# First stage of a one-layer transformer kernel: a load in two pieces, three weight subtractions on GpSimd, one subtraction later

## The chip, the cores and the metric

The kernel runs on one core of a Trainium2 chip. The metric is the device time of one execution in microseconds (us). Before the change it was 2847.78 us, the median of 3 runs (2846.89, 2847.78 and 2852.01 us).

The core has five engines with a queue of instructions each, and each queue runs strictly in its own order: PE (matrix products; PEld is its loading of weights), DVE (vector), ACT (scalar), POOL (GpSimd) and SP, which here issues all the DMA transfers. An instruction waits for semaphores of the engines or transfers that it depends on.

## The reference, cut to what matters

The program computes one layer: 2048 tokens of width 1024, stick-breaking attention with 16 heads, then a SwiGLU feed-forward network. Shift, scale and gate of each half come from a conditioning vector c.

```python
mod_all = jnp.einsum('bd,lde->lbe', jax.nn.silu(c), ada_w) + ada_b[:, None]
sh_m, sc_m, gt_m, sh_f, sc_f, gt_f = jnp.split(mod_all[i][:, None, :], 6, axis=-1)
h = modulate(rms_norm(x, norm_g[i, 0]), sh_m, sc_m)      # h * (1 + sc) + sh
y = stick_breaking_mixer(h, sb_w_qkv[r], sb_w_o[r])      # starts with h @ w_qkv
x = x + gt_m * rms_norm(y, norm_g[i, 1])
h = modulate(rms_norm(x, norm_g[i, 2]), sh_f, sc_f)
y = swiglu_ffn(h, ffn_w_in[i], ffn_w_out[i])
x = x + gt_f * rms_norm(y, norm_g[i, 3])
```

The change lies in the very beginning: the first shift and scale (`sh_m`, `sc_m`), the first 512 rows of `h`, and their product with the first 128 columns each of the q, k and v weights.

## The kernel before

All products are done to float32 accuracy by splitting each operand into a high part (rounded to the matrix engine's format) and a low part (the operand less its high part). `mm3` (lines 153 to 157) makes each product of three matmuls: high by high (L155), high weights by low activations (L156), low weights by high activations (L157). So every product needs two conversions, which ACT does, and two subtractions.

The first stage handles the first block of 512 tokens while the modulation vectors that it needs are themselves still being computed. Shift and scale (1024 values each) come in four pieces q = 0 to 3, each 256 values of both. A piece is a sum over 8 chunks of the conditioning vector, k = 0 to 7.

- Loads. `ada_chunk(q, kh)` loads the weights of piece q for half the chunks (kh = 0: chunks 0 to 3; kh = 1: chunks 4 to 7), 1 MB in one transfer of 8 KB per partition; piece 2 comes in eight transfers of 256 KB. `load_weights` loads a 128x1024 block of qkv weights (512 KB); t = 1, 0, 2 in the order of use (k, q, v).
- Sums. `ada_sum` (L639 for the first chunk, L642 for the others) adds one chunk times its value of c into `asum` on DVE. Chunk 7 (and chunk 0 of piece 0) skips DVE: `ada_direct` (L652) lets PE add it into the piece's accumulator `acol`; `ada_rest` (L659) lets PE add the columns of `asum`. `ada_cols_done` (L667, L669, L670) then makes `shift` and `g_eff` on DVE.
- First weights. `weights_high(t)` (L680) converts on ACT, `weights_low(t)` (L685) subtracts on DVE.
- First activations. `x_turn` transposes tile m of the normalised x on PE (L315). `full_high(m)` applies shift and scale on ACT (L701, tile `hf`) and converts it (L705, the high half of tile `ht`). `low(m)` subtracts (L710, the low half of `ht`) and, for odd m, puts the pair of tiles on a list of stores to `h_s`; these stores are issued at L405, during the next product but one.
- Products. `first_products(m, ts)` multiplies tile m with the weights t in `ts`; the order is 1, 0, 2.

The loop over q (from line 761) does for q = 0: begin piece 1, sum its chunks 0 to 6 on DVE, sum the first two chunks of piece 2, then on PE the products of tile 0, transposes, the direct and rest sums of piece 1, the products of tile 1, and last `ada_cols_done(1)` and `full_high` of tiles 2 and 3. For q = 1 and 2 the low parts of tiles 2q and 2q + 1 are put between the sums.

The queues of PE, ACT, DVE and POOL run in the order in which the program writes them. SP's order is the scheduler's. SP has eight semaphores for its transfers and uses them in turn, so a transfer is issued only when the one eight places before has landed.

Of the kernel before, what the change touches and what calls it, by code (L numbers as in the profile page):

```python
# [12 lines left out]
ALU = mybir.AluOpType  # L13
# [6 lines left out]
KC = D // P  # L20
# [61 lines left out]
def f32(ap):  # L82
    return ap.bitcast(F32)
# [3 lines left out]
def hybrid_trunk_kernel(  # L87
# [15 lines left out]
    nc = tc.nc  # L103
# [67 lines left out]
    def sb(shape, dtype, **kw):  # L171

        return (odd if kw["tag"] in ODD_TAGS else att).tile(shape, dtype, **kw)
# [3 lines left out]
    raws = {}  # L177

    def load_weights(p, t, tag="wraw"):
        raw = sb([P, KC, P], F32, name=f"wr{p}_{t}", tag=tag, bufs=BUFS[tag])  # L180
        nc.sync.dma_start(raw, wqkv[p, t])
        raws[p, t] = raw
# [110 lines left out]
    def x_load(b):  # L293
        for i in range(4):
            r0 = b * BT + i * P
            xt = sb([P, D], F32, name=f"x{b}_{i}", tag="v", bufs=BUFS["v"])
            nc.sync.dma_start(xt, x[r0 : r0 + P])
            x_tiles[b, i] = xt
# [11 lines left out]
    def x_turn(b, k):  # L310

        pool, tag = (tps, "t") if b < 2 else (accps, "acc")
        pt = pool.tile([P, BT], F32, name=f"xT{b}_{k}", tag=tag)
        for i in range(4):
            nc.tensor.transpose(  # L315
                pt[:, i * P : (i + 1) * P], x_norm[b, i][:, k * P : (k + 1) * P], ident
            )
        return pt
# [297 lines left out]
    def ada_chunk(q, kh):  # L616
        ks = range(KC // 2 * kh, KC // 2 * (kh + 1))
        if q == 2:
            for k in ks:
                w = sb([P, 2, AQ], F32, name=f"ac{q}_{k}", tag="a", bufs=BUFS["a"])  # L620
                nc.sync.dma_start(w, ada_first[q, kh][:, :, k % 4])
                chunks[q, k] = w
            return
        tag = "ht" if (q, kh) == (1, 1) else "qt"
        w = sb([P, 2, KC // 2, AQ], F32, name=f"ac{q}_{kh}", tag=tag, bufs=BUFS[tag])
        nc.sync.dma_start(w, ada_first[q, kh])
        for k in ks:
            chunks[q, k] = w[:, :, k % 4]

    def ada_begin(q):  # L630
        cols_ps[q] = zps.tile([P, BT], F32, name=f"acol{q}", tag="z")
        nc.vector.memset(cols_ps[q][:, :4], 0.0)

    def ada_sum(q, k):
        w, scale = chunks[q, k], c_act[:, k : k + 1]
        if q not in piece_sums:
            acc = sb([P, 2, AQ], F32, name=f"asum{q}", tag="w", bufs=BUFS["w"])
            piece_sums[q] = acc
            nc.vector.tensor_scalar(acc, w, scale, None, op0=ALU.mult)  # L639
        else:  # L640
            acc = piece_sums[q]
            nc.vector.scalar_tensor_tensor(acc, w, scale, acc, op0=ALU.mult, op1=ALU.add)  # L642

    def ada_sums(q):
        return [k for k in range(KC) if k not in ON_PE[q]]
# [3 lines left out]
    def ada_direct(q, k):  # L649

        for n, seg, js in COLUMNS:
            nc.tensor.matmul(  # L652
                cols_ps[q][:, n : n + 1], chunks[q, k][:, seg, js], c_act[:, k : k + 1],
                start=False, stop=False, skip_group_check=True,
            )

    def ada_rest(q):
        for n, seg, js in COLUMNS:
            nc.tensor.matmul(  # L659
                cols_ps[q][:, n : n + 1], piece_sums[q][:, seg, js], ones[:, 0:1],  # L660
                start=False, stop=n == 3, skip_group_check=True,
            )

    def ada_cols_done(q):

        ps, ms = cols_ps.pop(q), slice(2 * q, 2 * q + 2)
        nc.vector.tensor_tensor(shift[:, 0, ms], ps[:, 0:2], b_cols[:, 0, ms], op=ALU.add)  # L667
        sc = sb([P, KC], F32, name=f"sc0_{q}", tag="sc", bufs=1)[:, :2]
        nc.vector.tensor_tensor(sc, ps[:, 2:4], b_cols[:, 1, ms], op=ALU.add)  # L669
        nc.vector.scalar_tensor_tensor(  # L670
            g_eff[:, 0, ms], sc, 1.0, gc[:, 0, ms], op0=ALU.add, op1=ALU.mult
        )
# [5 lines left out]
    def weights_high(t):  # L678
        hl = sb([P, 2, KC, P], F32R, name=f"w0_{t}", tag="whl", bufs=BUFS["whl"])
        nc.scalar.copy(hl[:, 0], raws[0, t])  # L680
        weights[0, t] = hl[:, 0], hl[:, 1]

    def weights_low(t):
        hi, lo = weights[0, t]
        nc.vector.tensor_tensor(lo, raws.pop((0, t)), f32(hi), op=ALU.subtract)  # L685

    def first_products(m, ts=(1, 0, 2)):
        for t in ts:
            w = weights[0, t]
            mm3(  # L690
                first_acc[t], (w[0][:, m], w[1][:, m]),
                (first_h[m][:, 0], first_h[m][:, 1]), m == 0, m == KC - 1,
            )

    def full_high(m):
        if m % 2 == 0:
            ht = sb([P, 2, 2, BT], F32R, name=f"ht0_0_{m // 2}", tag="ht", bufs=BUFS["ht"])
            first_h.extend([ht[:, 0], ht[:, 1]])
            norm_tile[0] = ht
        full = sb([P, BT], F32, name=f"hf0_{m}", tag="tmp", bufs=BUFS["tmp"])  # L700
        nc.scalar.activation(  # L701
            full, turned_x.pop(m), AF.Identity,
            bias=shift[:, 0, m : m + 1], scale=g_eff[:, 0, m : m + 1],
        )
        nc.scalar.copy(first_h[m][:, 0], full)  # L705
        first_full[m] = full

    def low(m):
        hl = first_h[m]
        nc.vector.tensor_tensor(hl[:, 1], first_full.pop(m), f32(hl[:, 0]), op=ALU.subtract)  # L710
        if m % 2 == 1:
            stores.append((h_s[0][:, m - 1 : m + 1], f32(norm_tile[0])))
# [4 lines left out]
    nc.scalar.activation(spare, mhalf, AF.Sigmoid)  # L717
    x_load(0)
    ada_chunk(0, 0)
    ada_chunk(0, 1)  # L720
    load_weights(0, 1)
    nc.sync.dma_start(b_cols, ada_b_cols)
    nc.sync.dma_start(gc, g_cols)
    load_weights(0, 0)
    load_weights(0, 2, "qkn")
    ada_chunk(1, 0)
    ada_chunk(1, 1)
    ada_chunk(2, 0)
# [22 lines left out]
    ada_rest(0)  # L751
    weights_high(1)
    weights_low(1)
    ada_cols_done(0)
    weights_high(0)
    weights_low(0)
    weights_high(2)
    full_high(0)
    low(0)
    full_high(1)  # L760
    weights_low(2)
    low(1)


    for q in range(4):
        m = 2 * q
        if q < 3:
            if q == 0:
                ada_begin(1)
            begun = 2 if q > 0 else 0  # L770
            for n, k in enumerate(ada_sums(q + 1)[begun:]):
                ada_sum(q + 1, k)
                if q > 0 and n in (1, 3):
                    low(m + (n == 3))
            if q < 2:

                ada_begin(q + 2)
                for k in ada_sums(q + 2)[:2]:
                    ada_sum(q + 2, k)
        else:  # L780
            low(m)
            low(m + 1)
        first_products(m)
        if q < 3:
            turned_x[m + 2] = x_turn(0, m + 2)
            ada_direct(q + 1, KC - 1)
            if q == 0:
                first_products(m + 1, (1,))
            turned_x[m + 3] = x_turn(0, m + 3)
            ada_rest(q + 1)  # L790
            first_products(m + 1, (0, 2) if q == 0 else (1, 0, 2))
            ada_cols_done(q + 1)
            full_high(m + 2)
            full_high(m + 3)
        else:
            first_products(m + 1)
        if q == 1:
            load_weights(1, 1)
            load_weights(1, 0)
            x_load(1)  # L800
            load_weights(1, 2, "v")
# [595 lines left out]
    for n, (s, f) in enumerate(groups):  # L1397
# [3 lines left out]
        for at, product in enumerate(PRODUCTS):  # L1401
            acc = banks_of[{1: 0, 6: 0, 7: 0, 4: 0, 5: 1, 3: 1, 2: 2}[product]]
            for k in range(H4):
# [4 lines left out]
                t = 4 * at + k  # L1408
# [192 lines left out]
```

## Time and profile before

| | |
|---|---|
| time, median of 3 runs | 2847.78 us |
| time of the profiled execution | 2847.31 us |
| its span (first to last instruction) | 2845.1 us |
| PE busy | 2795.6 us, 98% of the span |
| DVE busy | 2028.4 us, 71% |
| ACT busy | 1632.3 us, 57% |
| POOL busy | 1277.0 us, 45% |
| DMA queue, share of 16 engines | 56.0% |
| L685 (low parts of the first weights), DVE | 3 of 128x1024, mean 1224 ns |
| L642 and L639 (sums of the pieces), DVE | 23 and 4 of 128x512 |

The profile is one execution; times in it are microseconds from the start of the span. In its timeline a row has the start, the time taken, the engine, the line, the operation, the tiles written and read (out<-in, numbers left out), the shapes, the count of merged instructions, and in brackets the idle time of the engine before it and what ended that. The profiled execution has 2.2 us outside its span.

### The profile page before, as it was taken

Reading aid. Unit: us, or ns where it says so; the run is one execution under the profiler, and the core shown is the slowest. Engines: PE = TensorE matmul, PEld = TensorE weight load, DVE = VectorE, ACT = ScalarE, POOL = GpSimd, SP = SyncE. Lnnn points to the kernel's source line nnn. Section 1 sums busy time; section 2 is a strip of 40 time slices with the busy share of each in tenths; the row PEclk is TensorE's granted clock in tenths of the full one; section 3 lists DMA queues with packets and bytes.
Section 4 is the critical chain, followed back from the end, with each engine's and each line's share of the span. In section 5 each row is a group of like instructions: output and inputs, shape, how many; then the busy total and the mean of one; then the engine's idle time right before and its main releaser. Section 6 shows DMA issues by size and latency. Waiting matters only on the chain.

```text
span 2845.1 us, 41790 instructions
## 1 busy us (share of the span) xinstructions
PE 2795.6 (98%) x13848; PEld 2333.9 (82%) x13848; DVE 2028.4 (71%) x2822; ACT 1632.3 (57%) x3265; POOL 1277.0 (45%) x2032
## 2 busy tenths in 40 slices
PE   7999999999999999999999999999999999999998
PEld 6788888888888888887888888888788888888887
DVE  6788898888888888888866766555775665133467
ACT  5787877788787877777645533333433333322243
POOL 1475666676576655656410122221222222544454
PEclk9999999999999999999999999999999999999999
DMA  8765556656665635546289645435453335545566
GB/s 329 271 211 167 189 155 227 211 170 234 189 209 192 209 118 179 196 133 231 88 299 312 203 137 152 122 98 161 130 177 108 112 107 163 191 142 155 180 214 195
DMA packets 239368, 516.84 MB, mean 182 GB/s; under 512 B 22321, under 2 KB 110385, under 8 KB 221489
## 3 DMA queue, kind: packets, MB, share of 16 engines
q1 hardware_dynamic: 239152, 514.18, 56.0%
q8 instruction: 109, 1.79, 0.3%
q14 instruction: 107, 0.87, 0.1%
HBM read 346.85 MB, written 118.49 MB: 164 GB/s over the span
## 4 chain that ended last, share of the span: by engine, by line
PE 87%; DVE 6%; ACT 2%; DMA 2%; issue 2%; POOL 1%; SPq 0%; DVEq 0%; POOLq 0%; ACTq 0%
PE s L155 9%; PE s L156 9%; PE s L157 9%; PE z L519 8%; PE o L598 8%; PE t L570 8%; PE pj L155 6%; PE pj L156 6%; PE pj L157 6%; PE o L156 4%; PE o L157 4%; PE o L155 4%; PE y L157 2%; PE y L155 2%; PE y L156 2%
## 5 line engine op out<-in xcount | busy, mean ns | idle before, releaser
L560 POOL TENSOR_TENSOR a<-a,w 128x512 f32<-128x512 f32 (+3 forms) x640 | 619.4, 968 | 217.8 <-DVE w L553 126.8
L553 DVE TENSOR_TENSOR_SCAN w<-z,c,begin 128x512 f32<-128x512 f32 x384 | 489.6, 1279 | 81.2 <-ACT z L538 61.5
L155 PE MATMUL s<-r,l 128*128 128x512 f32 x1232 | 481.4, 391 | 4.3 <-DVE p L1364 3.7
L157 PE MATMUL s<-r,l 128*128 128x512 f32 x1232 | 479.4, 389 | 0.0
L156 PE MATMUL s<-r,l 128*128 128x512 f32 x1232 | 479.3, 389 | 0.0
L536 ACT ACTIVATE a<-z 128x512 f32<-128x512 f32 (+3 forms) x640 | 347.2, 543 | 167.2 <-PE z L519 135.7
L598 PE MATMUL o<-aT,v 128*128 128x512 f32 (+3 forms) x1280 | 384.3, 381 | 0.1
L586 DVE TENSOR_TENSOR aT<-t,aT 128x512 fp32r<-128x512 f32 (+3 forms) x640 | 359.3, 596 | 22.9 <-ACT aT L580 22.2
L519 PE MATMUL z<-kt,qt 128*128 128x512 f32 (+3 forms) x1280 | 363.1, 365 | 0.0
L580 ACT CAST aT<-t 128x512 fp32r<-128x512 f32 (+3 forms) x640 | 314.1, 533 | 73.5 <-PE t L570 63.5
L538 ACT ACTIVATE z<-z 128x512 f32<-128x512 f32 (+3 forms) x640 | 344.8, 539 | 0.0
L1372 POOL TENSOR_TENSOR one<-p,p 128x512 f32<-128x512 f32 x44 | 70.5, 1602 | 577.8 <-issue 320.5
L155 PE MATMUL pj<-ht,w 128*128 128x512 f32 x768 | 309.7, 403 | 7.6 <-ACT ht L705 2.6
L156 PE MATMUL pj<-ht,w 128*128 128x512 f32 x768 | 302.0, 393 | 1.2 <-DVE ht L710 0.7
L570 PE MATMUL t<-begin,a 128*128 128x128 f32 x2176 | 294.8, 273 | 8.5 <-DVE aT L586 7.2
L570 PEld LDWEIGHTS t<-begin,a 128*128 128x128 f32 x2176 | 255.1, 140 | 58.0 <-DVE aT L586 10.8
L157 PE MATMUL pj<-ht,w 128*128 128x512 f32 x768 | 302.1, 393 | 0.0
L155 PEld LDWEIGHTS s<-r,l 128*128 128x128 f32 x1232 | 231.3, 188 | 54.4 <-ACT l L1225 2.9
L157 PEld LDWEIGHTS s<-r,l 128*128 128x128 f32 x1232 | 231.3, 188 | 48.2
L156 PEld LDWEIGHTS s<-r,l 128*128 128x128 f32 x1232 | 231.3, 188 | 47.9 <-issue 0.5
L548 DVE TENSOR_TENSOR_SCAN w<-z,begin 128x128 f32<-128x128 f32 (+3 forms) x256 | 208.8, 818 | 75.0 <-ACT z L538 62.2
L519 PEld LDWEIGHTS z<-kt,qt 128*128 128x128 f32 x1280 | 230.3, 188 | 37.4 <-DVE w L548 0.2
(160 smaller groups left out, 4865.8 us busy)
## 6 DMA issues: line engine op xcount, KB each, us to landing
ht<-h_s SPq DMA_DIRECT2D x108, 1024.0 KB, 8.1
wi<-in_win SPq DMA_DIRECT2D x86, 512.0 KB, 4.0
qt<-qn SPq DMA_DIRECT2D x124, 256.0 KB, 4.8
ol_qt<-act_s SPq DMA_DIRECT2D x56, 512.0 KB, 3.7
act_s<-S SPq DMA_DIRECT2D x66, 256.0 KB, 4.1
br<-in_wout SPq DMA_DIRECT2D x66, 256.0 KB, 3.6
h_s<-ht SPq DMA_DIRECT2D x16, 1024.0 KB, 7.8
o_s<-os SPq DMA_DIRECT2D x128, 128.0 KB, 2.4
```

Source lines behind the costliest of these rows:

```text
L155: nc.tensor.matmul(acc, lhs[0], rhs[0], start=first, stop=False, **kw)
L156: nc.tensor.matmul(acc, lhs[0], rhs[1], start=False, stop=False, **kw)
L157: nc.tensor.matmul(acc, lhs[1], rhs[0], start=False, stop=last, **kw)
L519: nc.tensor.matmul(z[:, :n], q[:, e, part, r * P : (r + 1) * P], k[:, e, :n], start=part == 0, stop=part == 1,)
L536: nc.scalar.activation(a[:, :n], z[:, :n], AF.Sigmoid, scale=QK_SCALE)
L538: nc.scalar.activation(z[:, :n], z[:, :n], AF.Sigmoid, scale=-QK_SCALE)
L553: nc.vector.tensor_tensor_scan(rest[:, rev], left[:, rev], begin[:, :BT][:, rev], initial=carries[r], op0=ALU.mult, op1=ALU.bypass,)
L560: nc.gpsimd.tensor_tensor(a[:, :n], a[:, :n], rest[:, 1 : n + 1], op=ALU.mult)
L570: nc.tensor.transpose(pt[:, rb * P : (rb + 1) * P], weighed[i, rb][:, j * P : (j + 1) * P], ident)
L580: nc.scalar.copy(hl[:, 0, t0:], pt[:, t0:])
L586: nc.vector.tensor_tensor(hl[:, 1, t0:], pt[:, t0:], f32(hl[:, 0, t0:]), op=ALU.subtract)
L598: nc.tensor.matmul(acc[:, t0:], lhs, hl[:, part, t0:], start=sc == qb and j == 0 and part == 0, stop=sc == 0 and j == 3 and part == 1,)
```

## The change

It has three parts. In `ada_chunk` the transfer of the second half of piece 0 becomes two transfers, chunks 4 and 5, then 6 and 7, each with two runs of 2 KB per partition. In `weights_low` the three subtractions go from DVE to GpSimd, and the third is written right behind the others. `low(1)` is taken out of the place behind `full_high(1)` and put into the loop of q = 0, behind chunk 3 of piece 1.

```diff
         w = sb([P, 2, KC // 2, AQ], F32, name=f"ac{q}_{kh}", tag=tag, bufs=BUFS[tag])
-        nc.sync.dma_start(w, ada_first[q, kh])
+
+        step = KC // 4 if (q, kh) == (0, 1) else KC // 2
+        for k in range(0, KC // 2, step):
+            nc.sync.dma_start(w[:, :, k : k + step], ada_first[q, kh][:, :, k : k + step])
...
     def weights_low(t):
         hi, lo = weights[0, t]
-        nc.vector.tensor_tensor(lo, raws.pop((0, t)), f32(hi), op=ALU.subtract)
+        nc.gpsimd.tensor_tensor(lo, raws.pop((0, t)), f32(hi), op=ALU.subtract)
...
     weights_high(2)
+    weights_low(2)
     full_high(0)
     low(0)
     full_high(1)
-    weights_low(2)
-    low(1)
...
             for n, k in enumerate(ada_sums(q + 1)[begun:]):
                 ada_sum(q + 1, k)
-                if q > 0 and n in (1, 3):
+                if n == 3 or q > 0 and n == 1:
                     low(m + (n == 3))
```

In the built program the orders of PE and ACT are the same as before. POOL has three instructions more and DVE three fewer. On SP the transfer count rises by one, and the first of the four stores to `h_s`, which stood behind the last load of the stage, now stands behind the eight transfers of `kn` and `qn` (L439, L453), next to the other three. Nothing else in the five orders differs.

## The prediction, made before the changed kernel ran

> **What bounds the kernel now.** I read the page first: the span, the busy times and the chain of waits.
>
> ```profile
> span 2845.1 us, 41790 instructions
> ...
> PE 2795.6 (98%) x13848; PEld 2333.9 (82%) x13848; DVE 2028.4 (71%) x2822; ACT 1632.3 (57%) x3265; POOL 1277.0 (45%) x2032
> ...
> PE 87%; DVE 6%; ACT 2%; DMA 2%; issue 2%; POOL 1%; SPq 0%; DVEq 0%; POOLq 0%; ACTq 0%
> ```
>
> PE is busy for 98% of the span and holds 87% of the chain. The time is therefore PE's work plus PE's idle time, and idle time is worth looking for only where the change acts. Later stages keep their order on every engine, so a microsecond won or lost in the first stage moves everything behind it, unless something else takes it up. The timeline of the first 40 us shows what the stage waits for.
>
> ```profile
> 11.41 1.83 PE L652 MATMUL acol<-c_act,ac 128*128 128x1 f32 x8 [11.41 <-DMA ac<-in_ada_first]
> ...
> 13.87 2.33 DVE L642 SCALAR_TENSOR_TENSOR asum<-ac,c_act,asum 128x512 f32<-128x512 f32 x3 [0.50 <-DMA ac<-in_ada_first]
> ...
> 14.85 1.71 PE L652 MATMUL acol<-c_act,ac 128*128 128x1 f32 x8
> 15.14 1.04 ACT L680 CAST w<-wr 128x1024 fp32r<-128x1024 f32 x1 [2.97 <-DMA wr<-in_wqkv]
> ...
> 16.42 1.84 PE L659 MATMUL acol<-ones,asum 128*128 128x1 f32 x8
> ...
> 17.79 1.04 ACT L680 CAST w<-wr 128x1024 fp32r<-128x1024 f32 x1 [0.22 <-DMA wr<-in_wqkv]
> ...
> 18.56 0.16 DVE L670 SCALAR_TENSOR_TENSOR g_eff<-sc,gc 128x2 f32<-128x2 f32 x1
> ...
> 18.82 0.78 ACT L701 ACTIVATE hf<-xT,shift,g_eff 128x512 f32<-128x512 f32 x1
> ...
> 20.28 0.69 DVE L710 TENSOR_TENSOR ht<-hf,ht 128x512 fp32r<-128x512 f32 x1 [0.41 <-ACT ht L705]
> ...
> 21.02 0.80 PE L156 MATMUL pj<-ht,w 128*128 128x512 f32 x1
> ...
> 22.02 0.69 DVE L710 TENSOR_TENSOR ht<-hf,ht 128x512 fp32r<-128x512 f32 x1
> ...
> 22.63 0.48 DVE L639 TENSOR_SCALAR asum<-ac,c_act 128x512 f32<-128x512 f32 x1
> ...
> 23.15 4.69 DVE L642 SCALAR_TENSOR_TENSOR asum<-ac,c_act,asum 128x512 f32<-128x512 f32 x6
> ...
> 25.72 0.39 PE L156 MATMUL pj<-ht,w 128*128 128x512 f32 x1
> ...
> 27.89 0.97 PEld L659 LDWEIGHTS acol<-ones,asum 128*128 128x128 f32 x8 [1.35 <-DVE asum L642]
> 27.89 1.05 PE L659 MATMUL acol<-ones,asum 128*128 128x1 f32 x8 [1.12 <-DVE asum L642]
> ...
> 29.50 0.78 ACT L701 ACTIVATE hf<-xT,shift,g_eff 128x512 f32<-128x512 f32 x1 [7.93 <-DVE g_eff L670]
> ```
>
> Two points set the pace. The first L701, at 18.82, needs `g_eff` (18.56 + 0.16 = 18.72) and also ACT's third conversion of weights (17.79 + 1.04 = 18.83): both come at once. Then DVE is the bound: it works without a break from 20.28 until the six L642 of piece 1 end at 23.15 + 4.69 = 27.84, and PE idles 1.12 us for them before L659. From there `g_eff`, L701 at 29.50 and the products of tile 2 follow. So the end of the sums of piece 1, 27.84, is the number to follow.
>
> **The change part by part.** *The split load.* Chunks 4 and 5 would land about halfway through the 1 MB, so the three L642 can start right behind the earlier ones, up to 0.50 us sooner (the idle time in their row), and end near 15.7. Nobody gains: L659 starts at 16.42 because PE's own L652 before it is modelled until 14.85 + 1.71 = 16.56, while the sums ended at 16.20. Gain 0 here, but DVE is clear of POOL's first subtraction. The runs of 2 KB are not in the trace; its neighbours are 8 KB (the first window) and 1 KB (the second).
>
> ```profile
> 9.00:13.50 4.50, 2.09 (x10) 2.12 (x11) 2.69 (x5) 3.14 (x4) 1.50 (x2) 1.00 1.02 426
> ...
> 23.60:28.60 5.00, 3.88 (x29) 3.28 (x28) 4.79 (x9) 0.00 (x0) 0.00 (x0) 1.00 1.11 362
> ```
>
> The last figure is GB/s: 1.05 MB takes 2.46 us at 426 and 2.90 us at 362, so everything queued behind it lands 0 to 0.44 us later; I take 0.2. ACT's three conversions wait for exactly those transfers, so L701 goes from 18.82 to about 19.05. The extra transfer also moves each later wait for a semaphore by one place, which costs nothing while the queue is full (426 GB/s).
>
> *The subtractions on POOL.* DVE loses three times 1.22 us (the mean in the next row), of which two lie after 20 us or just before it. What matters is what POOL and DVE do to each other, and the trace shows that elsewhere: first the timeline at 137, 618 and 2750 us, then the extremes of single lines (minimum/median/maximum in ns).
>
> ```profile
> L685 DVE TENSOR_TENSOR w<-wr,w 128x1024 fp32r<-128x1024 f32 x3 | 3.7, 1224 | 0.0
> ```
>
> ```profile
> 137.59 1.09 POOL L560 TENSOR_TENSOR a<-a,w 128x512 f32<-128x512 f32 x1
> 137.67 1.29 DVE L331 CAST ht<-hf 128x512 fp32r<-128x512 f32 x1 [0.28 <-ACT hf L325]
> ...
> 618.43 2.40 POOL L188 TENSOR_TENSOR w<-wr,w 128x1024 fp32r<-128x1024 f32 x1
> ...
> 620.11 1.29 DVE L219 SCALAR_TENSOR_TENSOR aacc<-aw,c_act,aacc 128x512 f32<-128x512 f32 x1
> ...
> 2749.74 3.61 DVE L1493 SCALAR_TENSOR_TENSOR xe<-tot,e_rstd,xe 128x512 f32<-128x512 f32 x2 [0.66 <-POOL e_rstd L846]
> 2750.41 2.39 POOL L1257 TENSOR_TENSOR ol_qt<-ol_qt 128x1024 fp32r<-128x1024 f32 x1 [0.71 <-DMA xe<-x_s]
> 2752.76 1.47 POOL L1257 TENSOR_TENSOR ol_aT<-ol_aT 128x384 fp32r<-128x384 f32 x1
> ```
>
> ```profile
> L188 POOL TENSOR_TENSOR w<-wr,w x21: 2379/2401/2420, 150.4 to 1156.5; 128x1024 fp32r<-128x1024 f32 x21
> ...
> L219 DVE SCALAR_TENSOR_TENSOR aacc<-aw,c_act,aacc x56: 724/730/1789, 357.6 to 2121.8; 128x512 f32<-128x512 f32 x56
> ...
> L331 DVE CAST ht<-hf x24: 393/427/1485, 65.5 to 145.3; 128x512 fp32r<-128x512 f32 x24
> ...
> L423 DVE TENSOR_TENSOR kn<-pj,kn x32: 665/682/693, 50.3 to 1301.4; 128x512 fp32r<-128x512 f32 x32
> ```
>
> L188 is the very operation that moves, on POOL: 2.40 us. Beside it L219, the same form as L642, took 1.29 us instead of 0.73 and ended 0.57 us after POOL did (621.40 against 620.83): it stood still until POOL was done. L331, which reads only one tile, was held too and ended 0.28 us after POOL. L423, which reads `pj` from the accumulators, never passes 693 ns. At 2750.41 POOL got in between two L1493 of DVE, and when it ended at 2752.80 the second L1493 went ahead of POOL's next operation, which took 1.47 us: they alternate. L710, L642, L639 and L670 read on-chip tiles alone, so all of them will be held.
>
> Now the three POOL operations, with 0.2 us of later landing. The first follows ACT's first conversion (15.14 + 1.04 + 0.2, and 0.08 from ACT to POOL): 16.47 to 18.87. L670 asks at 18.56, waits until 18.87 and goes next: done about 19.0, as late as ACT. The second runs 19.0 to 21.4. L710 asks near 20.5 and ends 0.55 behind POOL: 21.95 instead of 20.97. The third, waiting, runs 21.95 to 24.35. L639 is held and ends 0.33 behind it: 24.68 instead of 23.11. Then six L642 (4.69) and the second L710 between them (0.69 and some 0.03 of start): 24.72 + 4.69 + 0.72 = 30.13. Against 27.84 that is **+2.3 us**. Were L670 to lose its turn, the second would run at 18.87 to 21.27 and the third from 21.4 to 23.8; L710 would end at 24.35, L639 run free, and the sums end at 30.28, nearly the same: POOL's 7.2 us must pass either way. PE waits for the low part of tile 0 (about 1 us), of tile 1 and for the sums; all of it lies inside the 2.3. The third weights' low part is there at 24.35, when its L157 is due (23.91 + 1).
>
> Whether L639 is held rests on L331 alone. [...]
>
> *`low(1)` behind chunk 3.* It costs the same 0.69 us at another place. Without POOL it would let PE's L156 of tile 1 (25.72) wait for nothing, and here it is due at 27.7, ahead of the sums, hidden by their wait.
>
> *The moved store.* One store of 1 MB goes from where the DMA engines had nothing else to a full stretch.
>
> ```profile
> 33.86 0.33 SPq L405 DMA_DIRECT2D h_s<-ht  x1
> ...
> 56.11 4.15 SPq L405 DMA_DIRECT2D h_s<-ht  x3
> ```
>
> ```profile
> 48.00:50.00 2.00, 2.00 (x10) 1.69 (x9) 1.96 (x2) 1.55 (x3) 0.00 (x0) 1.00 0.00 0
> ...
> 72.00:74.00 2.00, 2.00 (x14) 1.70 (x13) 1.93 (x5) 1.31 (x3) 0.00 (x0) 1.00 0.56 229
> ```
>
> ```profile
> 75.08 7.82 DMA x<-in_x
> ```
>
> ```profile
> 85.00 0.33 PE L315 MATMUL xT<-begin,xn 128*128 128x128 f32 x1 [0.20 <-DVE xn L306]
> ```
>
> The next loads on which PE waits are those of x for the third block: the chain shows 7.82 us for the last of them from 75.08, and PE idles at 85. The store is 2.46 us of transfers at 426 GB/s. The queue ran partly empty at 72 to 74 (busy 0.56, so 0.9 us free, and 229 GB/s) before those loads were issued, which hides a part. Bounds 0 and +2.46; I take +0.3, near the lower one, since the loads are held by the order of issue (75.08) as well.
>
> Sum on the profiled execution's own time: 2847.31 + 2.3 + 0.3 = **2849.9 us**. The median of the runs is 0.47 above that execution, and the runs spread over 5.1 us. A change of under 0.2% (5.7 us) can hardly be told from none in this kernel, and this forecast, +0.09%, lies inside it.
>
> **The rivals.** *No holding (faster).* If DVE's instructions ran freely beside POOL, L710 would end at 21.2, and the sums at 21.2 + 0.48 + 4.69 + 0.72 = 27.1: a gain of 0.7, with the store 2846.9 us. For it: POOL works on other tiles than DVE. Against it: L219 at 1789 and L331 at 1485 ns.
>
> *The store in full.* If the loads of x land as much later as the store takes, PE's wait at 85 grows by 2.46 instead of 0.3: 2852.1 us. Against it: the free time at 72 to 74.
>
> *PE stays slow (slower beyond the bound).* PE starts slowly: eight small matmuls take 1.84 us at 16.42 and 1.05 at 27.89, one L156 0.80 at 21.02 and 0.39 at 25.72, all at a granted clock of 1.00 in the windows. New waits (0.7 us at 21, about 1.2 before the low part of tile 1 and before L659) cut up the stretch in which it became fast. If it stays slow through L659 and the six products behind it: 0.8 + 6 x 0.41 = 3.3 us, 2853.2. It decides from the point where the six products of tile 2 are slow as well: another 2.5, 2855.7 us, +0.28%. Against it: PE has some 3.5 us without a wait from 22.0, as long as it needed before. [...]
>
> **How the numbers follow.** Chances: the forecast 0.62 (2849.0 to 2850.8, by 0 to 0.44 for landings and 0.33 for L639), no holding 0.12, the store in full 0.10, PE slow 0.12, something not seen 0.04. The range 2846.3 to 2853.2 takes in the first four with PE slow up to its first point; left out are the rest of that case and half of the unseen. Slower by over 0.2% (above 2853.5): half of PE slow, what the store adds on top, and part of the unseen, 0.12. Faster by over 0.2%: no case reaches it, 0.04 for the unseen. Within: 0.84.
>
> **What would show it.** L710 of tile 0 at about 1.4 us and L639 at over 2 instead of 0.69 and 0.48; L659 of piece 1 starting near 30.2 after a longer idle time; L701 of tile 2 near 31.8; the first L701 near 19.05. Wrong if these DVE rows keep their times beside POOL, if L659 starts before 28, if the products from 25 on take 0.6 us or more each, or if PE's wait at 85 grows by over 1 us.

## The result and the profile after

| | before | changed |
|---|---|---|
| time, median of 22 runs each | 2848.68 us | 2853.85 us |
| lowest to highest | 2846.89 to 2854.3 | 2850.46 to 2857.64 |
| ratio, with its 95% interval | | 1.0016 (1.001 to 1.0023) |
| span of the profiled execution | 2845.1 us | 2852.5 us |

The changed kernel is slower by 0.16%, 2.8 to 6.6 us by the interval. The forecast was 2849.9 us, and the measured median lies 0.65 us above the forecast's range. The forecast was summed on a profiled execution of 2847.31 us, which lies 1.37 us below the median that the kernel before has here. As a difference the forecast was +2.6 us and the measured one is +5.2 us, so about half of the slowdown was foreseen. The change lies inside the 0.2% that was named as the bound for telling it from none; only the many runs show its sign.

The timeline of the changed kernel's first 40 us. Its line numbers are 3 higher around the functions in question: L642 is the first chunk's multiply (L639 before), L645 the other chunks' sums (L642), L662 the rest sum (L659), L673 `g_eff` (L670), L688 the subtraction of weights (L685), L704 the scaling on ACT (L701), L713 the subtraction of activations (L710).

```profile
16.72 7.43 POOL L688 TENSOR_TENSOR w<-wr,w 128x1024 fp32r<-128x1024 f32 x3 [5.70 <-ACT w L683]
...
18.81 0.28 DVE L673 SCALAR_TENSOR_TENSOR g_eff<-sc,gc 128x2 f32<-128x2 f32 x1
19.20 0.77 ACT L704 ACTIVATE hf<-xT,shift,g_eff 128x512 f32<-128x512 f32 x1
...
20.66 1.27 DVE L713 TENSOR_TENSOR ht<-hf,ht 128x512 fp32r<-128x512 f32 x1 [1.57 <-ACT ht L708]
21.86 2.57 DVE L642 TENSOR_SCALAR asum<-ac,c_act 128x512 f32<-128x512 f32 x1
...
29.69 1.54 PE L662 MATMUL acol<-ones,asum 128*128 128x1 f32 x8 [0.95 <-DVE asum L645]
...
31.78 0.78 ACT L704 ACTIVATE hf<-xT,shift,g_eff 128x512 f32<-128x512 f32 x1 [9.83 <-DVE g_eff L673]
...
39.03 0.95 PE L662 MATMUL acol<-ones,asum 128*128 128x1 f32 x8
```

DVE's rows on on-chip tiles are longer where POOL works, from 16.72 to 24.15: L713 takes 1.27 instead of 0.69 us, L642 2.57 instead of 0.48, even the tiny L673 0.28 instead of 0.16. L670 and L672, which read the accumulator `acol` in the same time, keep their 0.16 and 0.15. PE's rest sum of piece 1 starts at 29.69, where before it stood at 27.89: 1.80 us late. But the rest sum of piece 2, at 39.03, is later by twice that, as this row of the kernel before shows:

```profile
35.40 0.95 PE L659 MATMUL acol<-ones,asum 128*128 128x1 f32 x8
```

39.03 less 35.40 is 3.63 us. Between the two PE waited less than before (there 0.55 and 0.23 us for tile 2, here nothing); it was slower. The windows of the changed kernel show that, in their third column from the end, the granted clock:

```profile
26.68:30.09 3.41, 2.46 (x18) 2.05 (x18) 3.30 (x8) 0.00 (x0) 0.00 (x0) 1.00 1.09 390
30.09:33.50 3.41, 3.41 (x12) 2.93 (x13) 2.80 (x7) 1.69 (x3) 0.00 (x0) 0.50 1.01 418
33.50:36.92 3.42, 3.42 (x10) 2.56 (x9) 3.38 (x7) 1.00 (x2) 0.00 (x0) 0.50 1.02 410
```

PE had become fast at 26.68 and fell back to half the clock from 30.09 to 36.92. (The column does not show the slow start: it reads 1.00 before 26.68 as well, though a 128x512 product takes 0.63 us there, as long as at 0.50 later.) Then the third block. The queue of SP in the changed kernel, and PE's first transpose of that block:

```profile
59.31 5.34 SPq L405 DMA_DIRECT2D h_s<-ht  x4
...
76.11 4.31 SPq L297 DMA_DIRECT2D x<-in_x  x4
```

```profile
90.16 0.33 PE L315 MATMUL xT<-begin,xn 128*128 128x128 f32 x1 [1.80 <-DVE xn L306]
```

That transpose stood at 85.00 with 0.20 us of waiting; now it is at 90.16 after 1.80 us: 5.16 late, of which 1.5 is new. Near this wait the clock falls once more:

```profile
91.50:95.00 3.50, 3.30 (x9) 2.33 (x10) 2.31 (x4) 0.78 (x1) 0.00 (x0) 0.51 1.05 355
```

The spans differ by 7.4 us. So the profiled execution reads: 1.8 (DVE held, with 0.26 from a later first matmul, 11.67 against 11.41), 1.8 (clock at half), 1.5 (loads of x), and 2.3 behind them, among it the second fall of the clock. The medians differ by 5.2 only: the profiled execution of before is 1.4 below its median, and the profiled one of the changed kernel (2854.64) 0.8 above. The experiments take the causes apart.

### The profile page after: what moved, and what is told of

It is laid out like the page before. It is cut to its first block, busy times and chain, and to the rows that moved or that the text cites. A ratio compares the mean times of both kernels' runs of the same rounds, so it can differ in the third digit from the quotient of the medians.

```text
span 2852.5 us, 41795 instructions
## 1 busy us (share of the span) xinstructions
PE 2800.6 (98%) x13848; PEld 2337.8 (82%) x13848; DVE 2026.5 (71%) x2819; ACT 1631.2 (57%) x3265; POOL 1284.6 (45%) x2035
## 4 chain that ended last, share of the span: by engine, by line
PE 84%; DVE 6%; issue 3%; DMA 3%; ACT 2%; POOL 1%; SPq 0%; DVEq 0%; POOLq 0%; ACTq 0%
PE s L155 9%; PE s L157 9%; PE s L156 9%; PE z L519 8%; PE o L598 8%; PE t L570 8%; PE pj L155 6%; PE pj L156 6%; PE pj L157 6%; PE o L156 3%; PE o L155 3%; PE o L157 3%; PE y L157 1%; PE y L155 1%; PE y L156 1%
```

## The experiments

The theory after the result had three causes: DVE stands still while POOL subtracts; the store of `h_s` that moved in SP's queue delays the loads of x; PE's clock halves where the delays thin out its work. The rivals were the two other parts of the change and mere chance. Ratios are to runs of the kernel before on the same chip.

| kernel | subtractions | store of `h_s` | median us | before us | ratio (95%) |
|---|---|---|---|---|---|
| e1: split load alone | DVE | old place | 2849.8 | 2849.51 | 0.9999 (0.999 to 1.0007) |
| e3: `low(1)` alone | DVE | old place | 2848.98 | 2849.51 | 1.0 (0.9991 to 1.0009) |
| e2: POOL alone | POOL | late | 2855.3 | 2849.51 | 1.0019 (1.001 to 1.0029) |
| e5: changed, without POOL | DVE | late | 2851.03 | 2849.51 | 1.0008 (0.9999 to 1.0017) |
| e4: changed, store back | POOL | old place | 2853.14 | 2849.52 | 1.0008 (0.9998 to 1.0017) |
| e7: changed, PE filled | POOL | late | 2853.74 | 2849.52 | 1.0015 (1.0006 to 1.0024) |
| e8: e4 and e7 together | POOL | old place | 2850.25 | 2849.52 | 0.9997 (0.9989 to 1.0006) |
| e10: first subtraction on POOL | one of three | old place | 2848.81 | 2849.77 | 0.9995 (0.9986 to 1.0004) |
| e9: x loaded earlier, else before | DVE | old place | 2848.15 | 2849.52 | 0.9995 (0.9986 to 1.0004) |
| e11: e9 again | DVE | old place | 2846.97 | 2849.77 | 0.9993 (0.9984 to 1.0002) |
| e12: changed kernel again | POOL | late | 2855.32 | 2849.77 | one execution, no ratio |

### The parts one by one

The split load alone, on the kernel before:

```diff
-        nc.sync.dma_start(w, ada_first[q, kh])
+        step = KC // 4 if (q, kh) == (0, 1) else KC // 2
+        for k in range(0, KC // 2, step):
+            nc.sync.dma_start(w[:, :, k : k + step], ada_first[q, kh][:, :, k : k + step])
```

> The kernel before with the split load alone. Theory (three causes in the changed kernel: DVE held beside POOL, +1.8 us at the end of the sums of piece 1; the store behind the kn and qn transfers, +1.6 us at PE's wait near 85 us; the PE clock halved after longer waits, 1.1 to 1.5 us each time): none of them is here, the sums of piece 1 still end within 0.4 us of 27.84, the time is within 0.5 us of before. Rival (the runs of 2 KB push all later landings): the first L704 0.4 us or more later and the time 1 us or more above.

`low(1)` alone:

```diff
     weights_low(2)
-    low(1)
...
-                if q > 0 and n in (1, 3):
+                if n == 3 or q > 0 and n == 1:
```

> The kernel before with low(1) behind chunk 3 of piece 1, the third subtraction on DVE at its old place, the store of h_s at its old place. Theory: the DVE work up to the end of the sums is the same, so the sums end within 0.2 us of 27.84 and the time is within 0.5 us of before. Rival (PE's L156 of tile 1 now waits and the clock halves): 1 us or more above.

POOL alone:

```diff
-        nc.vector.tensor_tensor(lo, raws.pop((0, t)), f32(hi), op=ALU.subtract)
+        nc.gpsimd.tensor_tensor(lo, raws.pop((0, t)), f32(hi), op=ALU.subtract)
```

> The kernel before with the three subtractions on POOL alone, at their old places; its store of h_s stands behind the kn and qn transfers too. Theory: L710 and L639 are held as in the changed kernel, the sums of piece 1 end 1.8 to 2.3 us later, the last load of x for the third block lands 1.6 us later still, and the time is 3.5 to 7 us above before, as in the changed kernel. Rival (the parts only hurt together): under 2 us.

Split and `low(1)` each left the time as it was (the table's first two rows), as the theory said. POOL alone gave the whole slowdown, 1.0019; but its store of `h_s` had moved as well, so this run does not separate these two. Its timeline shows the two subtractions of activations, 0.69 us each, held together for 3.98, and the rest sum of piece 1 at 29.56, 1.7 us late (1.8 to 2.3 were expected); its windows show the clock at half near 30 and low again at 80 to 95.

```profile
16.38 7.45 POOL L685 TENSOR_TENSOR w<-wr,w 128x1024 fp32r<-128x1024 f32 x3 [5.48 <-ACT w L680]
...
20.39 3.98 DVE L710 TENSOR_TENSOR ht<-hf,ht 128x512 fp32r<-128x512 f32 x2 [1.56 <-ACT ht L705]
...
29.56 1.66 PE L659 MATMUL acol<-ones,asum 128*128 128x1 f32 x7 [1.37 <-DVE asum L642]
```

```profile
29.30:36.10 6.80, 6.54 (x19) 5.42 (x20) 5.79 (x13) 2.69 (x4) 0.00 (x0) 0.50 1.01 413
80.00:95.00 15.00, 12.38 (x49) 9.40 (x48) 6.32 (x14) 6.44 (x11) 2.90 (x5) 0.86 0.98 366
```

### One subtraction on POOL

```diff
+        eng = nc.gpsimd if t == 1 else nc.vector
-        nc.vector.tensor_tensor(lo, raws.pop((0, t)), f32(hi), op=ALU.subtract)
+        eng.tensor_tensor(lo, raws.pop((0, t)), f32(hi), op=ALU.subtract)
```

> The kernel before with the first of the three subtractions alone on POOL. Theory (what costs is POOL's subtraction while DVE has work on on-chip tiles): from 16.3 to 18.7 DVE has only the small L670 to do, which is held for 0.2 us at most, so the sums of piece 1 end within 0.3 us of 27.84 and the time is within 0.7 us of before. Rival (a subtraction of 2.35 us on POOL costs its 1.1 us more wherever it stands): the sums end 1 us later or more, and the time is 1 us or more above.

```profile
16.10 2.35 POOL L686 TENSOR_TENSOR w<-wr,w 128x1024 fp32r<-128x1024 f32 x1 [5.48 <-ACT w L680]
...
18.13 0.16 DVE L667 TENSOR_TENSOR shift<-acol,b_cols 128x2 f32<-128x2 f32 x1 [2.11 <-PE acol L659]
...
27.73 1.05 PE L659 MATMUL acol<-ones,asum 128*128 128x1 f32 x8 [0.42 <-DVE asum L642]
```

POOL is as slow as in the changed kernel (2.35 us), but DVE had 2.11 us with nothing to do just then, and the rest sum starts at 27.73, which is 16.48 us behind PE's first matmul, as in the kernel before. The time is not above before. So for this subtraction the slower engine costs nothing; what delays the sums in the changed kernel is the standing still of DVE where DVE has work. The same rows say that the change could not gain with this subtraction either: DVE's idle time there is no time that anyone waits for.

### The store

The changed kernel with the subtractions back on DVE; its store of `h_s` is still behind the `kn` and `qn` transfers:

```diff
-        nc.gpsimd.tensor_tensor(lo, raws.pop((0, t)), f32(hi), op=ALU.subtract)
+        nc.vector.tensor_tensor(lo, raws.pop((0, t)), f32(hi), op=ALU.subtract)
```

> The changed kernel with the three subtractions back on DVE, in the changed order; its store of h_s still stands behind the kn and qn transfers. Theory: no DVE row is held, the sums of piece 1 end within 0.5 us of 27.84, but the last load of x for the third block lands about 1.6 us later against PE, and PE's wait near 85 us grows by that: the time is 1.5 us above before, up to 3 if the clock halves behind that wait. Rival (the held DVE rows are the whole cause): within 0.5 us of before.

The changed kernel with the store at its old place:

```diff
             load_weights(1, 2, "v")
+            nc.sync.dma_start(*stores[0])
...
-                if parked and t == 1 and k % 2 == 0:
+                if parked and t == 1 and k in (2, 4, 6):
```

> The changed kernel with the first store of h_s issued at its old place, behind the last load of the stage. Theory: DVE rows are held and the sums of piece 1 end 1.8 us late as in the changed kernel, but PE's wait for the third block's x near 85 to 88 us is as short as before (0.2 us for its first transpose): 1.8 us above before plus up to 1.5 where the clock halves near 30 us, so 1.8 to 3.3 above. Rival (the store has no part in it): 4 to 5 us above before, as the changed kernel.

PE's first transpose of the third block, first in e5 and then in e4:

```profile
87.37 0.33 PE L315 MATMUL xT<-begin,xn 128*128 128x128 f32 x1 [1.73 <-DVE xn L306]
```

```profile
86.96 0.33 PE L315 MATMUL xT<-begin,xn 128*128 128x128 f32 x1 [0.18 <-DVE xn L306]
```

With the store late the wait is 1.73 us although no DVE row is held; with the store at its place it is 0.18 although they are. The wait follows the store and not the held rows. In time, e5 is 1.5 us above before by medians, as expected, with an interval that just reaches no change. E4 is 2.3 us above by its ratio, inside the 1.8 to 3.3 that was expected, and 3.6 by medians, a little above; its interval reaches no change too (0.9998).

### The clock

The changed kernel with eight more transposes of data that PE already has, in its wait for the sums:

```diff
             turned_x[m + 3] = x_turn(0, m + 3)
+            if q == 0:
+                for _ in range(2):
+                    for i in range(4):
+                        nc.tensor.transpose(turned_x[m + 3][...], x_norm[0, i][...], ident)
             ada_rest(q + 1)
```

> The changed kernel with eight more transposes on PE (tile 3 of x transposed twice more, into the same place) ahead of the rest sum of piece 1, where PE waits 0.96 us. Theory: the clock falls at 30 us because that stretch has too little work; with the filler it stays up there, PE is 1.0 to 1.5 us ahead of the changed kernel from 37 us on, and the time is 3 to 3.8 us above before. Rival (the clock falls on its own schedule): the granted clock still falls near 30 us and the time stays 4.5 to 5 us above before.

Two windows of e7 behind the first rise of the clock:

```profile
24.94:28.35 3.41, 3.08 (x23) 2.54 (x22) 3.30 (x6) 0.00 (x0) 0.00 (x0) 1.00 1.15 369
28.35:31.76 3.41, 3.22 (x23) 2.60 (x20) 3.27 (x10) 0.71 (x1) 0.00 (x0) 1.00 1.00 414
```

The clock stayed up, and the rest sum of piece 2 starts at 36.94 instead of 39.03 (0.25 of it is an earlier first matmul). The time fell less than expected: 4.2 us above before by medians, 1.0015 by the ratio, which can't be told from the changed kernel's 1.0016. The effect is shown in the trace; its size in an average execution is not.

Filler and store together, the edits of e7 and e4:

> The changed kernel with both: the store at its old place and the eight filling transposes. Theory: only the held DVE rows are left, 1.8 to 2.2 us above before. Rival (a further cost that neither touches): 3 us or more above before.

That brings the time back to before (0.9997, up to 1.0006). 1.8 to 2.2 us were expected to be left. The trace of e8 keeps a part of them, with PE's first transpose of the third block at 86.52 against 85.00, but the time shows less than was expected, at most 1.7 us by the interval. I can't settle where the rest is regained. Two comparisons among these runs, all on one chip, are of use. E7 and e8 differ in the store alone, and e7 is 3.5 us above by medians, all its runs but one above all of e8's. E4 and e8 differ in the filler alone; e4 is 2.9 us above by medians, but their runs overlap widely. So the store is the part that the times show best; why it costs more in this pair than the 1.5 us of its wait is not shown.

The changed kernel itself, once more:

> The changed kernel itself, one more execution with a profile. Theory: the clock falls in the first window behind its first rise again (near 30 us), since the same stretch has the same waits; PE is 3 us or more late by 37 us. Rival (the fall came by chance): the granted clock stays 1.00 until 60 us and PE is 2 us late.

```profile
29.44 1.05 PE L662 MATMUL acol<-ones,asum 128*128 128x1 f32 x8 [1.06 <-DVE asum L645]
```

```profile
30.00:40.00 10.00, 9.64 (x43) 7.53 (x42) 6.86 (x14) 2.69 (x4) 0.00 (x0) 0.66 1.02 409
```

The rest sum starts at 29.44, and the mean clock from 30 to 40 us is 0.66: the fall came again, one window later than expected. Its rest sum of piece 2 stands at 39.34. This execution is the best comparison for e7: PE became fast at the same time in both (24.8 and 24.9 us), and behind this window, without the filler, the clock fell where in e7 it stayed up:

```profile
28.25:31.66 3.41, 2.35 (x16) 1.94 (x14) 3.27 (x10) 0.61 (x1) 0.00 (x0) 1.00 1.02 419
```

The fall near 30 us came in all four profiles with the three subtractions on POOL and no filler (two of the changed kernel, e2, e4) and in none of the profiles of before, e1, e3, e5, e7, e8, e9 and e10. The later fall, between 87 and 98 us, is less clear: it came in all five profiles with the late store, but also in e3 and e8, where the store is at its old place and PE's wait is 0.18 us; in before, e1, e4 and e9 PE's products up to 95 us show none. That the store's wait sets it off is therefore not shown.

### A version from the finding

If stores in front of the loads of x set PE's wait, the loads can go ahead of the next store. The kernel before with that edit alone:

```diff
+                    if k == 0 and nb and nb > 1:
+                        x_load(nb)
                     if p == 0:
                         first_norm(b, k + 3)
-                    if k == 0 and nb and nb > 1:
-                        x_load(nb)
```

> The kernel before with the loads of x for the third and fourth block issued one store of h_s earlier in the queue. Theory (stores in front of the loads of x set PE's wait at 85 us): the last load for the third block lands by 79 instead of 82.9 us, PE's waits for its first transposes shrink from 1.2 us in all to under 0.5, the time is 1 to 2.5 us below before. Rival (ACT's squares, not the loads, end that wait): within 0.5 us of before.

> The kernel with the loads of x issued one store earlier, once more, for its interval: theory 0.5 to 2 us below before, by the 1.24 us that PE gained near 86 us; rival: within 0.5 us of before, the gain given back later.

```profile
69.08 3.16 SPq L297 DMA_DIRECT2D x<-in_x  x4
```

```profile
85.72 0.33 PE L315 MATMUL xT<-begin,xn 128*128 128x128 f32 x1 [0.33 <-DVE xn L306]
```

The loads are issued at 69.08, where the kernel before has them at 72.58, and of PE's four waits at the third block's first transposes, 1.2 us in all, one of 0.33 us is left. So this wait follows the loads, as the theory said. By medians e9 and e11 are 1.4 and 2.8 us below before, but each interval holds no change (up to 1.0004 and 1.0002). It is the likely best version and not a proven one.

## Why the prediction was wrong

**What bounds the stage: right.** The end of the sums of piece 1 set PE's pace. L662 followed them. That L704 of tile 2 came at 31.78, where 31.8 was forecast, is partly luck: the sums ended at 29.64 and not at 30.13, and L662 behind them took 1.54 us instead of 1.05 because the clock fell.

**The split load: right.** No gain was forecast and about 0.2 us of later landing; alone it changed nothing (0.9999), and the first L704 at 19.20 is 0.38 later, of which 0.26 is the later start of that execution (the first matmul starts anywhere between 11.25 and 11.71 us, with the split or without).

**DVE held beside POOL: right in mechanism, nearly in size.** Forecast: L713 about 1.4 us, L642 over 2, the sums' end 2.3 later. Measured: 1.27, 2.57 and 1.8, the last with the 0.26 of the later start in it. L642, with its one input, was held too: it ended 0.28 us behind POOL (24.43 against 24.15). The range allowed 0.33 us for L639 running free; no run shows it beside POOL at its own 0.48 us, and the changed kernel and e12 have 2.57. PE's idle time before L662 was forecast to grow; it shrank from 1.12 to 0.95, since PE itself came later.

**The moved store: mis-sized, the first step that failed.** The term was +0.3, taken near the lower bound of 0 to 2.46, "since the loads are held by the order of issue (75.08) as well". PE's wait grew by 1.6 (0.20 to 1.80), and e5 shows it without POOL. The free time at 72 to 74 was filled, but it covers no more than its own length. The prediction's own figures, 2.46 us of transfers less 0.9 us free, make 1.56 us, an estimate that the measured 1.5 to 1.6 bears out. The order of issue gave no further cover. In the changed kernel, where PE is 3.6 us later, the DMA engines have no free time left ahead of the loads:

```profile
73.53:75.53 2.00, 2.00 (x14) 1.65 (x13) 1.24 (x3) 1.64 (x3) 0.00 (x0) 1.00 1.06 434
75.53:77.53 2.00, 2.00 (x14) 1.71 (x13) 1.93 (x5) 1.30 (x3) 0.00 (x0) 1.00 0.99 416
```

SP begins to issue the four loads no later against PE than before (76.11 less 72.58 is 3.53), but the issue takes 4.31 us instead of 3.10 and the last load lands 8.13 us after its issue instead of 7.82. These rows are the issue in the kernel before and the last landing in the changed one:

```profile
72.58 3.10 SPq L297 DMA_DIRECT2D x<-in_x  x4
```

```profile
79.93 8.13 DMA x<-in_x
```

**The clock: left out of the sum, the second step that failed.** "PE stays slow" had 0.12, for the reason that PE "has some 3.5 us without a wait from 22.0, as long as it needed before". The traces show no such length: from PE's last wait until it was fast it took 2.6 us in the kernel before (21.02 to 23.57) and 4.7 us in the changed one (21.98 to 26.68). It did become fast in time; that it could fall back afterwards was not considered. Both profiles of the changed kernel have that fall. The length of PE's wait alone does not explain it: PE idles 0.95 us before the rest sum here and 0.70 in e4, where the clock falls, and 1.12 in the kernel before, where it stays up. The price of the case was 3.3 us, or 5.8 with the products of tile 2 slow as well, as they then were. It was too high: between the two rest sums the trace shows 1.8 us, and 2.4 in e12. The price took the rows' durations, 0.41 us more for each product, but the rows overlap. Their starts, first at half clock in the changed kernel and then at full clock before, lie 0.42 and 0.24 us apart, so a product costs 0.2 us more; and PE's waits for tile 2 took up a part.

```profile
32.52 0.63 PE L155 MATMUL pj<-ht,w 128*128 128x512 f32 x1
...
32.94 0.63 PE L156 MATMUL pj<-ht,w 128*128 128x512 f32 x1
```

```profile
32.29 0.40 PE L155 MATMUL pj<-ht,w 128*128 128x512 f32 x1
...
32.53 0.40 PE L156 MATMUL pj<-ht,w 128*128 128x512 f32 x1
```

**The sum.** With +1.8 for the hold, +1.5 for the store and +1.8 for the clock the terms give 5.1 us, and the measured difference of medians is 5.2. That they agree so well is partly luck: the terms come from one pair of profiled executions, whose times differ by 7.3, and e8, which keeps the hold alone, is at most 1.7 us above before. The steps that failed are the cover assumed for the store (+0.3 in the sum, 1.5 to 1.6 in the trace) and the clock, which the sum put at nothing (1.8 in the trace). The hold that was argued most was nearly right as a delay of the stage; that it costs as much in the whole time is not shown.

## What to carry to other kernels

Before moving an elementwise operation from DVE to GpSimd, list what DVE does in the same microseconds: if those are operations on on-chip tiles, DVE can stand still until POOL's operation ends (L642 ended 0.28 us behind POOL), and the move can cost the stage more than it frees (here 7.4 us of POOL for 3.7 of DVE). Compare the order of the transfers in the built program as well: a store that slips behind a burst is paid for by the next loads in the queue, and free time in the queue covers only its own length of it (here 2.46 us of store at 426 GB/s, 0.9 us free, and 1.5 to 1.6 us more at PE's wait). Work of PE that is thinned out on a critical stretch can cost twice, once as idle time and once as clock (in the changed kernel 0.95 us before the rest sum, and 1.8 us lost at a granted clock of 0.50 behind it).

## What the runs showed of the hardware

The granted clock moved in steps of 3.41 us and only between 1.00 and 0.50: in the changed kernel it was 0.50 from 30.09 to 36.92, two steps, and from 91.53 to 94.95, one, and 1.00 in the sixteen steps between. The steps do not begin with the kernel: PE became fast at 23.57 us in the kernel before, at 26.68 and 24.84 in the two profiles of the changed one, and at 27.3 in e5. The clock fell behind windows in which PE was busy for 2.46 of 3.41 us (the changed kernel) and for 2.71 (e4, first row), and it did not fall in the kernel before behind a window with 2.50 (second row):

```profile
27.20:30.61 3.41, 2.71 (x21) 2.30 (x20) 3.30 (x7) 0.00 (x0) 0.00 (x0) 1.00 1.08 409
```

```profile
26.98:30.39 3.41, 2.50 (x14) 1.94 (x14) 3.27 (x10) 0.86 (x2) 0.00 (x0) 1.00 1.07 410
```

PE's busy time alone therefore doesn't decide it. The number of large matmuls (128x512) in the window doesn't decide it either: the clock fell behind three in the changed kernel and behind six in e12 (28.25 to 31.66), and it stayed up behind three in e10 and behind the six of the second row above. The measure stays open. The falls near 90 us came in executions of the changed kernel and of others (0.50 from 88.70 to 92.10 in e5). They are likely one source of the spread between runs; that was not tested.
